# RG-LRU layer of a four-layer trunk: another form of the input scale, later gates, and one weight pool for the whole layer

## The chip, the core and the metric

The kernel runs on one core of a Trainium2 chip. The metric is the device time of one launch in microseconds (us), taken as the median of several runs. The engines are named as in the profile: PE (TensorE, matrix multiplication), PEld (its weight loads), DVE (VectorE), ACT (ScalarE), POOL (GpSimd), and SP, whose queue issues all the DMAs of this kernel.

## The reference

One step of a trunk with four layers and 384 tokens (128 of context, then 256 latents), width 1024. Each layer is a token mixer, a normalisation, a gated ConvFFN and another normalisation. The mixers are gated DeltaNet (layers 0 and 3), Mamba-2 SSD (layer 1) and RG-LRU (layer 2). Everything is float32. The change touches layer 2's mixer, whose core is:

```
def lru_mixer(h, s0, w_in, w_conv, conv_b, gate_w, gate_b, lam, w_out):
    gate_branch, xr = jnp.split(h @ w_in, 2, axis=-1)              # 1280 channels each
    xr = dwconv1d(xr, w_conv) + conv_b                             # 4 taps along the tokens
    gates = jnp.einsum('btnk,dgnkm->btdgnm', xr.reshape(b, t, 10, 128), gate_w)
    gates = jax.nn.sigmoid(gates.reshape(b, t, 2, 2, 1280) + gate_b)
    r, i = gates[:, :, :, 0], gates[:, :, :, 1]                    # for two directions
    log_a = -8.0 * r * jax.nn.softplus(-lam)
    bx = jnp.sqrt(-jnp.expm1(2.0 * log_a)) * i * xr[:, :, None]
    a = jnp.exp(log_a)
    y, s_fin = bidirectional(linear_scan, (a fwd, bx fwd), (a bwd, bx bwd), s0)   # h = a h + bx
    y = y * jax.nn.gelu(gate_branch)
    return y @ w_out, s_fin
```

The kernel before writes 1 - a^2 as (1 + a^2) tanh(-log a), and the kernel after takes its root from (1 + a)^2 tanh(-log(a)/2).

## The kernel before

**Number format and weights.** Every float32 product is made of three matmuls on halves: a weight `w` becomes `wh` (rounded, written by ACT at L111) and `wl = raw - wh` (POOL or DVE at L120), and the activations are split in the same way. `wload` does it: a DMA into a `raw` tile, the ACT copy, the subtraction. A pool on the right side of the memory holds a number of `raw` tiles and of `wh`/`wl` pairs. `WBUFS` gives these two numbers for the mixers of kind 0, 1 and 2 (gated DeltaNet, SSD, RG-LRU), and its last entry is for the output projection and the FFN. SSD has 3 `raw` tiles and 4 pairs, RG-LRU has 4 and 3. The loads of the modulation weights (`ada`, 512 KB each) that run beside the mixer take tiles of the same `raw` ring.

**Order.** The program is written for a framework that places the tiles, sets the semaphores and orders the instructions of each engine by the program order and by its own estimates of time; once made, each engine's order is fixed and runs in sequence. `keep_in_program_order` pins some ACT instructions.

**The mixer `lru`.** Ten blocks of 128 channels. `proj` goes through 20 projections of 24 matmuls of 128x384: x0-x3, z0-z2, x4-x6, z3-z5, x7-x9, z6-z9, each into one of two banks of accumulators `psc`. For an x block, `conv4` (one ACT instruction, then six of DVE at L117) makes `xr`, which is split into `xh` and `xl`; for a z block a copy brings it into `gb` (DVE at L765). `proj` yields four times per projection, and at each yield the generators in `post` go one step. `gates(n, ...)` waits two steps, then makes four gate products of three matmuls each, with sigmoids by ACT into `R` (the r gates) and `Iv` (the i gates), and multiplies `Iv` by `xr`, on POOL for odd n.

After each group of x blocks `scans` runs: `decay(n)` makes tanh and exp of `log a` on ACT (pinned), then on DVE and POOL the product (1 + a^2) tanh(-log a) in `th`; ACT takes the root; `scan(n)` multiplies `Iv` by `th`, runs four scans (L688), copies the final states into `st` (L691) and adds the two directions. When the z blocks of the group are there, a GELU on `gb` and a product give y.

**Output projection.** `outproj` multiplies the split y (`yh`, `yl`) with ten weights, k = 0 to 9. The first three weights are loaded at the end of `proj` from the mixer's own pool; then this pool is closed and another, `WBUFS[3]` = (2, 6), is opened for the rest of the layer. The last four k wait in `late` and are multiplied token tile by token tile in `boundary`, together with the normalisation. Before that, four weights of the FFN are fetched ahead from the same pool. Only y0 is split into a tile of the outer pool; the others have six `yh`/`yl` pairs of a pool that is opened when the mixer's inner pool has been closed.

Of the kernel before, what the change touches and what calls it, by code (L numbers as in the profile page):

```python
# [9 lines left out]
AF = mybir.ActivationFunctionType  # L10
ALU = mybir.AluOpType
# [4 lines left out]
NT = 384  # L16
# [9 lines left out]
SIDE = 4, 4, 4  # L26
FENCE = 4
HOSTED = ((6, 2, 1), (3, 2, 1), (3, 0, 1), (2, 1, 0))
WBUFS = ((4, 2), (3, 4), (4, 3), (2, 6))


C_ID, C_MU, C_ML, C_SG = 0, 128, 256, 384
# [52 lines left out]
class Trunk:  # L85
# [425 lines left out]
    def outw(self, wsrc, k):  # L511
        return self.wload(wsrc[k], lo_eng=self.nc.vector if k % 2 else self.nc.gpsimd)

    def outproj(self, l, nk, wsrc, gety, tail=4, ws=(), swap=False):

        pts = self.acc6()
        late, y = [], gety(0)
        for k in range(nk):
            if k == nk - tail - 1:
                self.open_bnd(l, 0)  # L520
            w = ws[k] if k < len(ws) else self.outw(wsrc, k)
            nxt = gety(k + 1) if k + 1 < nk else None
            if k < nk - tail:
                for t in range(3):
                    for half in range(2):
                        self.out_mm(pts[t][half], t, half, w, y, k == 0, False)
            else:
                late.append((k, w, y))
            if swap and k == len(ws) - 1:
                self.close_w()  # L530
                self.open_w(*WBUFS[3])
            y = nxt
        self.prefetch([self.I["ffn_in"][l, i % 2 * NFF + i // 2] for i in range(4)])
        self.boundary(l, 0, pts, late, nk)
# [18 lines left out]
    def ffn(self, l):  # L553
# [3 lines left out]
        with tc.tile_pool(name=self.nm("ffn"), bufs=1, reuse_waits="tile") as fp:  # L557
# [57 lines left out]
            if not last:  # L615
                self.open_w(*WBUFS[self.next_layer(l) % 3])
                self.prefetch(self.first_srcs(self.next_layer(l)))
# [3 lines left out]
    def lru(self, l, j):  # L621
        nc, tc, I = self.nc, self.tc, self.I
        NB = 10
        done, post = set(), []
        with ExitStack() as es:
            op = es.enter_context(tc.tile_pool(name=self.nm("lru"), bufs=1, reuse_waits="tile"))
            Iv = self.sb(op, [128, NB, 2, NT], "I")
            gb = self.sb(op, [128, NB, NT], "gb")
            flat = gb.rearrange("p n t -> p (n t)")
            lpool = tc.tile_pool(name=self.nm("lru1"), bufs=1, reuse_waits="tile")  # L630
            lp = self.adap = lpool.__enter__()
            cw = self.sb(op, [128, NB, 5], "cw")
            sm = self.sb(op, [128, NB, 8], "sm")
            sa = self.sb(op, [128, NB, 2], "sa")
            st = self.sb(op, [128, NB, 2], "st")
            R = None

            def small():
                self.load(cw, I["lru_conv"])
                self.load(sm, I["lru_small"])  # L640
                nl = self.sb(op, [128, NB, 2], "nl")
                self.ts(nl, sm[:, :, 4:6], -1.0, ALU.mult)
                out = []
                for _ in self.softplus(op, nl, [128, NB, 2], "sp", out):
                    pass
                sp = out[0]
                self.ts(sa, sp, -8.0, ALU.mult)

            def gates(n, xr, xs, wg):
                for _ in range(2):  # L650
                    yield
                for q in range(4):
                    s = slice(q * 128, (q + 1) * 128)
                    pg = self.ps("b")
                    self.mm3(pg[:, :NT], (wg[0][:, s], wg[1][:, s]), xs, True, True)
                    dst = (R, Iv)[q % 2][:, n, q // 2, :]
                    self.act(dst, pg[:, :NT], AF.Sigmoid, 1.0, sm[:, n, q:q + 1])
                    yield
                iv = Iv[:, n, :, :]
                self.tt(iv, iv, xr.unsqueeze(1).to_broadcast([128, 2, NT]), ALU.mult, (nc.vector, nc.gpsimd)[n % 2])  # L660
                done.add(("gate", n))

            ths, ys = {}, []

            def gety(pool, n, bufs):
                yh, yl = (self.sb(pool, [128, NT], t, bufs, F32R) for t in ("yh", "yl"))
                self.split(yh, yl, Iv[:, n, 0, :])
                return yh, yl

            def decay(n):  # L670
                r = R[:, n, :, :]
                th = ths[n] = self.sb(lp, [128, 2, NT], "th", 4)
                for f in (AF.Tanh, AF.Exp):
                    for d in range(2):
                        dst = th if f == AF.Tanh else r
                        tc.keep_in_program_order(self.act(dst[:, d, :], r[:, d, :], f, sa[:, n, d:d + 1]))
                u = self.sb(lp, [128, 2, NT], "u", 2)
                self.ts(th, th, -1.0, ALU.mult, 1e-30, ALU.max)
                self.tt(u, r, r, ALU.mult, nc.gpsimd)
                self.stt(th, u, 1.0, th, ALU.add, ALU.mult)  # L680

            def scan(n):
                r, iv = R[:, n, :, :], Iv[:, n, :, :]
                self.tt(iv, iv, ths[n], ALU.mult)
                for d in range(2):
                    for si, (a, b) in enumerate(SEGS):
                        rng = slice(a, b) if d == 0 else slice(b - 1, a - 1 if a else None, -1)
                        nc.vector.tensor_tensor_scan(  # L688
                            out=iv[:, d, rng], data0=r[:, d, rng], data1=iv[:, d, rng],
                            initial=sm[:, n, 6 + d:7 + d] if si else 0.0, op0=ALU.mult, op1=ALU.add)  # L690
                nc.vector.tensor_copy(st[:, n, :], iv.rearrange("p d t -> p (d t)")[:, 127:NT + 1:NT - 127])  # L691
                self.tt(iv[:, 0, :], iv[:, 0, :], iv[:, 1, :], ALU.add)

            def scans(ns, zs):
                while not all(x in done for x in [("gate", n) for n in ns] + [("scan", n) for n in range(ns[0])]):
                    yield
                for n in ns:
                    decay(n)
                    yield
                    yield  # L700
                for n in ns:
                    tc.keep_in_program_order(self.act(ths[n], ths[n], AF.Sqrt))
                    yield
                for n in ns:
                    scan(n)
                    done.add(("scan", n))
                    yield
                while ("z", zs[-1]) not in done:
                    yield
                g = gb[:, zs[0]:zs[-1] + 1, :]  # L710
                tc.keep_in_program_order(self.act(g, g, AF.Gelu_apprx_tanh))
                for n in zs:
                    y = Iv[:, n, 0, :]
                    self.tt(y, y, gb[:, n, :], ALU.mult)
                    if n == 0:
                        ys.append(gety(op, 0, 1))
                    yield

            def proj():
                nonlocal R  # L720
                parts = (range(4), range(3)), (range(4, 7), range(3, 6)), (range(7, NB), range(6, NB))
                seq = [(k, n) for p in parts for k, ns in zip("xz", p) for n in ns]
                lo = nc.gpsimd, nc.vector
                first = self.first_pair([I["lru_in"][NB + k] for k in range(2)])
                small()
                affine = self.affine(flat[:, :D], flat[:, D:2 * D])
# [4 lines left out]

                def gate_w(n):
                    if n < NB:
                        return self.wload(I["lru_gate"][n], 512, ("gwh", "gwl"), 2, lp, lo[n % 2])

                gw, nxt = gate_w(0), None
                for i, (kind, n) in enumerate(seq):
                    w = nxt
                    if i < 2:
                        pt = first[i]  # L740
                        if i:
                            nxt = weights(2)
                    else:
                        pt = self.ps("c")[:, :NT]
# [7 lines left out]
                    for _ in range(2):  # L752
                        next(affine, 0)
                    if kind == "x":
                        xr = self.sb(lp, [128, NT], "xr", 3)
                        self.conv4(pt, xr, cw[:, n, 0:4], cw[:, n, 4:5])
                        xh = self.sb(lp, [128, NT], "xh", 3, F32R)
                        xl = self.sb(lp, [128, NT], "xl", 3, F32R)
                        self.split(xh, xl, xr)
                        if R is None:  # L760
                            R = self.sb(lp, [128, NB, 2, NT], "R")
                        post.append(gates(n, xr, (xh, xl), gw))
                        gw = gate_w(n + 1)
                    else:
                        nc.vector.tensor_copy(gb[:, n, :], pt)  # L765
                        done.add(("z", n))
                    for ns, zs in parts:
                        if (kind, n) == ("x", ns[-1]):
# [2 lines left out]
                while self.fillers:  # L771
                    self.fill()
                    yield
                for k in range(3):
                    ws.append(self.outw(I["lru_out"], k))
                self.close_h()

            ws = []
            self.interleave([], proj(), post, [], None, done, 1.0, None)
            lpool.__exit__(None, None, None)  # L780
            kpool = es.enter_context(tc.tile_pool(name=self.nm("lru2"), bufs=1, reuse_waits="tile"))
            self.outproj(l, NB, I["lru_out"], lambda n: gety(kpool, n, 6) if n else ys[0], ws=ws, swap=True)
            with tc.issue_after(self.last_load.ins):
                self.load(self.O["lru"], st)

# [1032 lines left out]
```

## Time and profile before

| What | Value |
|---|---|
| Time, median of 3 runs | 2821.39 us (2820.75 to 2823.31) |
| The profiled execution | 2822.25 us, its span 2820.5 us |
| PE, PEld busy | 2603.0 us (92%), 2315.0 us (82%) |
| DVE, ACT, POOL busy | 1968.2 us (70%), 1328.0 us (47%), 1302.6 us (46%) |
| Granted clock of TensorE, mean | 0.968 |
| Layer 2's mixer, from its first matmul to the FFN's first | 1512.5 to 1765.2 us of the span |

The busy times are sums over stages that differ. An engine's row in the chain of waits, or what a wait of PE ended on, tells more than its share. A line such as L117 is that of a helper which records one kind of operation for the whole kernel (L105 a matmul, L111 an activation, L117 scalar_tensor_tensor, L120 tensor_tensor, L124 tensor_scalar, L134 a DMA), so the tile names tell what a row is. In a list of groups the columns are: engine, operation, out<-in, shape, count, then busy time in all and mean ns of one, then the idle time of the engine ahead of them and what ended it.

### The profile page before, as it was taken

The numbers are of one execution on the slowest core, as the hardware profiler recorded it, in microseconds if no ns is written. First come the engines' busy times: TensorE is split into PE (matmuls) and PEld (weight loads), VectorE is DVE, ScalarE is ACT, GpSimd is POOL, SyncE is SP. The second block draws the span as 40 slices with busy tenths as digits, with TensorE's granted clock in tenths as the row PEclk, the third lists the DMA queues.
The fourth block names the chain that finished last, engine by engine and source line by source line (L and its number), as shares of the span: only waits on it lengthen the run. The fifth ranks groups of instructions, "written<-read, shape, count | busy, mean of one in ns | idle before, by whom it ended". The sixth has DMA issues, their size and how long they took to land. (4 is left out here: it accounts for less than half of the span.)

```text
span 2820.5 us, 43591 instructions
## 1 busy us (share of the span) xinstructions
PE 2603.0 (92%) x16376; PEld 2315.0 (82%) x16376; DVE 1968.2 (70%) x4240; ACT 1328.0 (47%) x2304; POOL 1302.6 (46%) x730
## 2 busy tenths in 40 slices
PE   6899999999989998999998777999979999899997
PEld 3798887799977887779997675899969989778996
DVE  3766655787787676378777776787776665578777
ACT  2456545434335566343434564344345555544443
POOL 1443432456544334345664653456546434335663
PEclk8999999999999999999999998999999999899998
DMA  7532314544444342554445443334442112153442
GB/s 256 177 100 92 111 63 161 174 130 135 149 163 152 119 129 78 187 169 135 136 144 170 156 140 111 119 127 138 160 144 90 53 59 62 36 185 121 150 134 84
DMA packets 114643, 366.47 MB, mean 130 GB/s; under 512 B 13760, under 2 KB 25728, under 8 KB 114432
## 3 DMA queue, kind: packets, MB, share of 16 engines
q1 hardware_dynamic: 114432, 363.67, 39.9%
q8 instruction: 130, 2.13, 0.3%
q14 instruction: 81, 0.66, 0.1%
HBM read 357.78 MB, written 5.84 MB: 129 GB/s over the span
## 5 line engine op out<-in xcount | busy, mean ns | idle before, releaser
L120 POOL TENSOR_TENSOR wl<-raw,wh 128x1024 fp32r<-128x1024 f32 x305 | 737.5, 2428 | 858.1 <-ACT wh L111 821.8
L105 PE MATMUL psc<-hh,wh 128*128 128x384 f32 x2168 | 759.9, 351 | 55.7 <-DVE xr L117 16.2
L117 DVE SCALAR_TENSOR_TENSOR acc<-psc,cw,acc 128x189 f32<-128x189 f32 (+3 forms) x1680 | 646.2, 412 | 164.6 <-ACT acc L111 131.2
L105 PE MATMUL psc<-hh,wl 128*128 128x384 f32 x2168 | 738.1, 340 | 3.4 <-POOL wl L120 3.4
L105 PE MATMUL psc<-hl,wh 128*128 128x384 f32 x2168 | 735.8, 339 | 0.0
L105 PEld LDWEIGHTS psc<-hh,wh 128*128 128x128 f32 x2168 | 413.8, 191 | 100.8 <-issue 69.7
L111 ACT ACTIVATE wh<-raw 128x1024 fp32r<-128x1024 f32 x345 | 362.4, 1053 | 264.9 <-PE psc L105 51.2
L105 PEld LDWEIGHTS psc<-hl,wh 128*128 128x128 f32 x2168 | 414.5, 191 | 5.7 <-issue 2.4
L105 PEld LDWEIGHTS psc<-hh,wl 128*128 128x128 f32 x2168 | 412.9, 190 | 7.0 <-POOL wl L120 5.1
L120 POOL TENSOR_TENSOR wol<-raw,woh 128x1024 fp32r<-128x1024 f32 x88 | 211.8, 2407 | 160.9 <-ACT woh L111 159.8
L111 ACT ACTIVATE gh<-g 128x384 fp32r<-128x384 f32 x88 | 46.2, 525 | 329.0 <-DVE g L120 329.0
L111 ACT ACTIVATE acc<-psc,cw 128x384 f32<-128x384 f32 x168 | 96.6, 575 | 191.7 <-PE psc L105 191.7
L120 POOL TENSOR_TENSOR PB<-M,cst 128x512 fp32r<-128x512 f32 x96 | 128.2, 1350 | 112.1 <-PE psa L105 110.1
L111 ACT ACTIVATE V<-psa 128x512 fp32r<-128x512 f32 x144 | 84.9, 595 | 133.7 <-PE psa L105 133.2
L105 PE MATMUL psa<-woh,gl 128*128 128x512 f32 x352 | 137.1, 391 | 3.6 <-DVE gl L120 3.6
L105 PE MATMUL psa<-woh,gh 128*128 128x512 f32 x352 | 137.5, 391 | 0.2 <-ACT gh L111 0.2
L105 PE MATMUL psa<-wol,gh 128*128 128x512 f32 x352 | 137.6, 391 | 0.0
L105 PE MATMUL psa<-raw,csilu 128*32 128x256 f32 x1216 | 106.4, 418 | 28.3 <-DMA raw<-in_ada_w 28.1
L111 ACT ACT_TABLE_LOAD x66 | 84.7, 1283 | 36.0 <-DVE kT L117 12.0
L120 DVE TENSOR_TENSOR wl<-raw,wh 128x1024 fp32r<-128x1024 f32 x40 | 54.3, 1358 | 59.2 <-ACT wh L111 58.9
L111 ACT ACTIVATE woh<-raw 128x1024 fp32r<-128x1024 f32 x88 | 92.6, 1052 | 0.0
L120 DVE TENSOR_TENSOR gl<-g,gh 128x384 fp32r<-128x384 f32 x88 | 53.7, 610 | 52.3 <-ACT gh L111 52.3
(341 smaller groups left out, 5163.3 us busy)
## 6 DMA issues: line engine op xcount, KB each, us to landing
raw<-in_ffn_in SPq DMA_DIRECT2D x176, 512.0 KB
raw<-in_ada_w SPq DMA_DIRECT2D x152, 512.0 KB
raw<-in_ffn_out SPq DMA_DIRECT2D x88, 512.0 KB
raw<-in_gdn_in SPq DMA_DIRECT2D x66, 512.0 KB
araw<-in_ada_w SPq DMA_DIRECT2D x40, 512.0 KB
raw<-in_ssd_in SPq DMA_DIRECT2D x25, 512.0 KB
raw<-in_lru_in SPq DMA_DIRECT2D x20, 512.0 KB
raw<-in_gdn_out SPq DMA_DIRECT2D x16, 512.0 KB
```

What stands on the lines that cost most here:

```text
L105: return self.nc.tensor.matmul(out, l, r, start=start, stop=stop, skip_group_check=True)
L111: x = self.nc.scalar.activation(out, in_, f, scale=scale, bias=bias, **kw)
L117: return self.nc.vector.scalar_tensor_tensor(out=out, in0=a, scalar=s, in1=b, op0=op0, op1=op1)
L120: return (eng or self.nc.vector).tensor_tensor(out=out, in0=a, in1=b, op=op)
```

## The change

Six edits to layer 2's mixer:

1. `decay` takes tanh(-log(a)/2) with a second column of factors `sh`, and multiplies `Iv` by (1 + a) itself. The negation with its lower bound (L124), the square `u` on POOL and the product with `th` go; the root is taken of the tanh alone.
2. The z blocks are copied by ACT, not DVE.
3. `gates` begins four steps behind its projection, not two. `R` is a ring of seven tiles of one block instead of one tile for all, and `xr` has two tiles, not three.
4. `Iv` times `xr` is on DVE for every block; the lower halves of the gate weights are on POOL for every block; the copy into `st` is on POOL.
5. y0, y1 and y2 are split into tiles of the outer pool as soon as they are made.
6. RG-LRU's pool has 3 `raw` tiles and 5 pairs and is kept to the end of the layer, the FFN included (`swap` is gone); four output weights are fetched at the end of `proj`, not three.

```diff
-WBUFS = ((4, 2), (3, 4), (4, 3), (2, 6))
+WBUFS = ((4, 2), (3, 4), (3, 5), (2, 6))
...
-            if swap and k == len(ws) - 1:
-                self.close_w()
-                self.open_w(*WBUFS[3])
             y = nxt
...
                 self.ts(sa, sp, -8.0, ALU.mult)
+                self.ts(sh, sp, 4.0, ALU.mult)
 
             def gates(n, xr, xs, wg):
-                for _ in range(2):
+                for _ in range(4):
                     yield
+                R[n] = self.sb(lp, [128, 2, NT], "R", 7)
...
-                self.tt(iv, iv, xr.unsqueeze(1).to_broadcast([128, 2, NT]), ALU.mult, (nc.vector, nc.gpsimd)[n % 2])
+                self.tt(iv, iv, xr.unsqueeze(1).to_broadcast([128, 2, NT]), ALU.mult)
...
             def decay(n):
-                r = R[:, n, :, :]
+                r, iv = R[n], Iv[:, n, :, :]
                 th = ths[n] = self.sb(lp, [128, 2, NT], "th", 4)
-                for f in (AF.Tanh, AF.Exp):
-                    for d in range(2):
-                        dst = th if f == AF.Tanh else r
-                        tc.keep_in_program_order(self.act(dst[:, d, :], r[:, d, :], f, sa[:, n, d:d + 1]))
-                u = self.sb(lp, [128, 2, NT], "u", 2)
-                self.ts(th, th, -1.0, ALU.mult, 1e-30, ALU.max)
-                self.tt(u, r, r, ALU.mult, nc.gpsimd)
-                self.stt(th, u, 1.0, th, ALU.add, ALU.mult)
+                for d in range(2):
+                    tc.keep_in_program_order(self.act(th[:, d, :], r[:, d, :], AF.Tanh, sh[:, n, d:d + 1]))
+                for d in range(2):
+                    tc.keep_in_program_order(self.act(r[:, d, :], r[:, d, :], AF.Exp, sa[:, n, d:d + 1]))
+                self.stt(iv, r, 1.0, iv, ALU.add, ALU.mult)
...
-                nc.vector.tensor_copy(st[:, n, :], iv.rearrange("p d t -> p (d t)")[:, 127:NT + 1:NT - 127])
+                nc.gpsimd.tensor_copy(st[:, n, :], iv.rearrange("p d t -> p (d t)")[:, 127:NT + 1:NT - 127])
                 self.tt(iv[:, 0, :], iv[:, 0, :], iv[:, 1, :], ALU.add)
...
-                    if n == 0:
-                        ys.append(gety(op, 0, 1))
+                    if n < 3:
+                        ys[n] = gety(op, n, 3)
...
-                        return self.wload(I["lru_gate"][n], 512, ("gwh", "gwl"), 2, lp, lo[n % 2])
+                        return self.wload(I["lru_gate"][n], 512, ("gwh", "gwl"), 2, lp)
...
-                        xr = self.sb(lp, [128, NT], "xr", 3)
+                        xr = self.sb(lp, [128, NT], "xr", 2)
...
-                        if R is None:
-                            R = self.sb(lp, [128, NB, 2, NT], "R")
...
-                        nc.vector.tensor_copy(gb[:, n, :], pt)
+                        self.act(gb[:, n, :], pt, AF.Copy)
...
-                for k in range(3):
+                for k in range(4):
                     ws.append(self.outw(I["lru_out"], k))
...
-            self.outproj(l, NB, I["lru_out"], lambda n: gety(kpool, n, 6) if n else ys[0], ws=ws, swap=True)
+            self.outproj(l, NB, I["lru_out"], lambda n: ys.get(n) or gety(kpool, n, 6), ws=ws)
```

More of the change, by code (lines that the diff above doesn't have):

```diff
@@ L512, in outw, with outproj @@
         return self.wload(wsrc[k], lo_eng=self.nc.vector if k % 2 else self.nc.gpsimd)
-    def outproj(self, l, nk, wsrc, gety, tail=4, ws=(), swap=False):
+    def outproj(self, l, nk, wsrc, gety, tail=4, ws=()):
         pts = self.acc6()
@@ L634, in lru @@
             sa = self.sb(op, [128, NB, 2], "sa")
+            sh = self.sb(op, [128, NB, 2], "sh")
             st = self.sb(op, [128, NB, 2], "st")
-            R = None
+            R = {}
             def small():
@@ L655, in gates @@
                     self.mm3(pg[:, :NT], (wg[0][:, s], wg[1][:, s]), xs, True, True)
-                    dst = (R, Iv)[q % 2][:, n, q // 2, :]
+                    dst = Iv[:, n, q // 2, :] if q % 2 else R[n][:, q // 2, :]
                     self.act(dst, pg[:, :NT], AF.Sigmoid, 1.0, sm[:, n, q:q + 1])
@@ L659, in gates @@
                 iv = Iv[:, n, :, :]
-                self.tt(iv, iv, xr.unsqueeze(1).to_broadcast([128, 2, NT]), ALU.mult, (nc.vector, nc.gpsimd)[n % 2])
+                self.tt(iv, iv, xr.unsqueeze(1).to_broadcast([128, 2, NT]), ALU.mult)
                 done.add(("gate", n))
-            ths, ys = {}, []
+            ths, ys = {}, {}
             def gety(pool, n, bufs):
@@ L670, in decay @@
             def decay(n):
-                r = R[:, n, :, :]
+                r, iv = R[n], Iv[:, n, :, :]
                 th = ths[n] = self.sb(lp, [128, 2, NT], "th", 4)
-                for f in (AF.Tanh, AF.Exp):
-                    for d in range(2):
-                        dst = th if f == AF.Tanh else r
-                        tc.keep_in_program_order(self.act(dst[:, d, :], r[:, d, :], f, sa[:, n, d:d + 1]))
-                u = self.sb(lp, [128, 2, NT], "u", 2)
-                self.ts(th, th, -1.0, ALU.mult, 1e-30, ALU.max)
-                self.tt(u, r, r, ALU.mult, nc.gpsimd)
-                self.stt(th, u, 1.0, th, ALU.add, ALU.mult)
+                for d in range(2):
[3 more added lines that the diff above has]
+                self.stt(iv, r, 1.0, iv, ALU.add, ALU.mult)
             def scan(n):
-                r, iv = R[:, n, :, :], Iv[:, n, :, :]
+                r, iv = R[n], Iv[:, n, :, :]
                 self.tt(iv, iv, ths[n], ALU.mult)
@@ L714, in scans @@
                     self.tt(y, y, gb[:, n, :], ALU.mult)
-                    if n == 0:
-                        ys.append(gety(op, 0, 1))
+                    if n < 3:
+                        ys[n] = gety(op, n, 3)
                     yield
             def proj():
-                nonlocal R
                 parts = (range(4), range(3)), (range(4, 7), range(3, 6)), (range(7, NB), range(6, NB))
                 seq = [(k, n) for p in parts for k, ns in zip("xz", p) for n in ns]
-                lo = nc.gpsimd, nc.vector
                 first = self.first_pair([I["lru_in"][NB + k] for k in range(2)])
```

## The prediction

> **What bounds the kernel now.** I read the busy times by stage first, then what PE waited for in each stage, then the chain of work that ended last, then the groups. The stage table is for the whole mixer and four parts of it; its columns are busy time (and count) of PE, PEld, DVE, ACT and POOL, then TensorE's granted clock.
>
> ```profile
> core 0: us, PE busy (x) PEld busy (x) DVE busy (x) ACT busy (x) POOL busy (x), PEclk, DMA share, GB/s
> 1537.00:1708.00 171.00, 129.56 (x728) 109.32 (x726) 131.31 (x186) 104.34 (x156) 95.10 (x47) 0.92 0.43 139
> 1571.00:1624.00 53.00, 35.21 (x207) 29.68 (x205) 48.60 (x67) 32.65 (x48) 31.50 (x16) 0.94 0.44 137
> 1624.00:1667.00 43.00, 33.80 (x202) 29.33 (x202) 35.79 (x52) 27.96 (x40) 22.13 (x10) 0.92 0.51 161
> 1690.00:1708.00 18.00, 10.19 (x30) 7.04 (x29) 18.00 (x28) 9.01 (x12) 5.09 (x2) 0.77 0.23 81
> 1708.00:1749.00 41.00, 37.28 (x139) 28.74 (x139) 17.34 (x22) 12.31 (x14) 12.11 (x5) 0.89 0.41 132
> ```
>
> The reader is to see that DVE is all but full from 1571 to 1624 (48.6 of 53) and wholly full from 1690 to 1708, while PE stands at two thirds and about half. The chain of waits between 1571 and 1710 says the same: the scans, the products on `I` and the two operations on `th` lead it, all on DVE.
>
> ```profile
> by line: DVE I L688 19.2%; DVE I L120 15.4%; DVE th L117 11.4%; DVE th L124 7.2%; DVE xr L117 6.8%; POOL wl L120 4.2%; PE psb L105 4.1%; DVE st L691 3.5%; POOL u L120 3.4%; DVE gwl L120 3.3%; PE psc L105 3.3%; DVE xl L120 3.2%; DMA raw<-in_
> ```
>
> So what the mixer can gain is what PE waits for. First from 1571 to 1690 (the projections), then from 1690 to 1749 (the output projection); the columns are the total, the times and the longest.
>
> ```profile
> PE psc L105 <- DVE xr L117: 16.2, 5, 5.1
> PE psb L105 <- DVE xl L120: 5.4, 2, 3.8
> PE psc L105 <- POOL wl L120: 3.0, 2, 2.8
> PE psc L105 <- DVE gb L765: 2.7, 2, 2.5
> ```
>
> ```profile
> PE psa L105 <- DVE yl L120: 5.0, 1, 5.0
> PE psa L105 <- ACT wh L111: 3.1, 2, 1.8
> PE psa L105 <- POOL wl L120: 2.7, 2, 1.7
> ```
>
> Together 27.3 us in the first and 10.8 us in the second. To these comes time at a lower clock: length times (1 - clock) is 3.2 and 3.4 us in the second and third rows of the table, 4.1 and 4.5 us in the last two, 15.2 us at most, since part of it was idle anyhow.
>
> **The work that is removed and moved.** The groups on DVE and POOL from 1537 to 1708:
>
> ```profile
> L117 DVE SCALAR_TENSOR_TENSOR th<-u,th 128x768 f32<-128x768 f32 x10 | 17.9, 1794 | 5.7 <-POOL u L120 5.3
> ...
> L124 DVE TENSOR_SCALAR th<-th 128x768 f32<-128x768 f32 x10 | 14.4, 1435 | 13.2 <-ACT th L111 13.1
> ...
> L120 DVE TENSOR_TENSOR I<-I,xr 128x768 f32<-128x768 f32 x5 | 6.7, 1348 | 6.7 <-ACT I L111 6.6
> L120 DVE TENSOR_TENSOR gwl<-raw,gwh 128x512 fp32r<-128x512 f32 x4 | 6.6, 1651 | 0.0
> L120 DVE TENSOR_TENSOR I<-I 128x384 f32<-128x384 f32 x10 | 6.3, 630 | 0.0
> L691 DVE COPY st<-I 128x2 f32<-128x2 f32 x10 | 5.7, 565 | 0.0
> L765 DVE COPY gb<-psc 128x384 f32<-128x384 f32 x10 | 5.5, 548 | 1.4 <-PE psc L105 1.4
> ```
>
> ```profile
> L120 POOL TENSOR_TENSOR u<-R 128x768 f32<-128x768 f32 x10 | 16.7, 1670 | 6.4 <-ACT R L111 6.4
> L120 POOL TENSOR_TENSOR x<-x,gb 128x512 f32<-128x512 f32 x9 | 13.8, 1553 | 0.0
> L120 POOL TENSOR_TENSOR I<-I,xr 128x768 f32<-128x768 f32 x5 | 11.6, 2327 | 4.7 <-ACT I L111 4.7
> L120 POOL TENSOR_TENSOR gwl<-raw,gwh 128x512 fp32r<-128x512 f32 x4 | 6.6, 1657 | 3.8 <-ACT gwh L111 3.8
> ```
>
> DVE loses the negation (14.4), the gate weights' lower halves (6.6), the state copies (5.7) and the z copies (5.5), 32.2 us, and gains five products with `xr` at 1.35, 6.7 us. The product (1 + a) on `Iv` has the count and shape of the one on `th` that goes. Net 25.5 of 131.3 us, a fifth. The views of the tiles `th` and `st` give minimum, median and maximum in ns:
>
> ```profile
> L124 DVE TENSOR_SCALAR th<-th x10: 548/1466/2756, 1571.5 to 1688.1; 128x768 f32<-128x768 f32 x10
> L117 DVE SCALAR_TENSOR_TENSOR th<-u,th x10: 943/2018/2944, 1575.5 to 1689.0; 128x768 f32<-128x768 f32 x10
> ```
>
> ```profile
> L691 DVE COPY st<-I x10: 132/136/2286, 1598.7 to 1705.2; 128x2 f32<-128x2 f32 x10
> ```
>
> A copy of two elements takes 0.13 or 2.29 us: the long ones stand behind POOL's work. So POOL's load counts twice. It loses 28.3 us (`u` and its products with `xr`) and gains some 7 us of gate weights and ten tiny copies. Without `u` the new product may fall from 1.79 to 0.94 us, 8.5 us more; I count none of that apart.
>
> **Terms in the projections, 1571 to 1690.**
> - The `xr` waits (16.2 us): PE lacks an accumulator bank because `conv4` stands in DVE's queue behind the `th` chain and the scans. Between nothing and 16.2; a fifth of DVE's work goes, and the rounds ACT-DVE-POOL-DVE-ACT ahead of the root too, so I take 10.
> - The `xl` waits (5.4): with four steps, about one projection, between split and gate products, I take 5. Each gate ends two steps later; behind the last come four z projections, which hide that for PE.
> - The z copies (2.7): ACT frees the bank now, but in its own queue. Nearest row, an ACT read of the same shape from PSUM:
>
> ```profile
> L111 ACT ACTIVATE R<-psb,sm 128x384 f32<-128x384 f32 x20 | 11.4, 576 | 16.3 <-PE psb L105 16.1
> ```
>
>  ten times 0.58 is 5.8 us on an engine with 104.3 of 171 busy; between -2.7 and +5.8, I take -2, as the row is as short as DVE's.
> - POOL's `wl` (3.0): POOL is lighter by about 20 of 95 us; I take 1.
> - Clock: 3 of the 6.6 us here.
>
> That is -21.
>
> **The price of three `raw` tiles.** This speaks against the change. Loads issued between 1518 and 1674.4 us:
>
> ```profile
> raw<-in_ada_w SPq DMA_DIRECT2D x22, 512.0 KB
> raw<-in_lru_in SPq DMA_DIRECT2D x18, 512.0 KB
> raw<-in_lru_gate SPq DMA_DIRECT2D x8, 256.0 KB
> ```
>
> 48 loads in 156.4 us through four tiles: a tile is held for up to 13.0 us (DMA, ACT's copy, POOL's subtraction, and any wait for a free pair). With three, the same length needs 9.8 us. The SSD mixer has three, and from 855 to 899 us, 44 us long, it issued 16 full loads:
>
> ```profile
> raw<-in_ssd_in SPq DMA_DIRECT2D x9, 512.0 KB
> raw<-in_ada_w SPq DMA_DIRECT2D x7, 512.0 KB
> ```
>
> 2.75 us a load, a hold of 8.25. At that pace the 48 loads take 132 us (no price); at an unchanged hold 208 us (+52). The SSD row is the nearer, since two more pairs let a `raw` tile go earlier; but POOL is busier here. I take +5, counting the first projections (1512 to 1571), where nothing else changes for PE. The projections thus gain 16.
>
> **Terms in the output projection, 1690 to 1749.** Before, the second pool held everything up:
>
> ```profile
> 1719.23 13.64 SPq L134 DMA_DIRECT2D raw<-in_lru_out  x5
> ```
>
> ```profile
> 1716.47 0.52 ACT L111 ACTIVATE yh<-I 128x384 fp32r<-128x384 f32 x1 [4.84 <-PE psb L105]
> 1716.90 1.99 ACT L111 ACTIVATE wh<-raw 128x1024 fp32r<-128x1024 f32 x2
> ```
>
> The last five loads start at 1719.2, after ACT, stuck behind a `yh` copy, has made the halves of k = 3 and 4. After the change three y are ready when the z blocks end, four weights are on their way, and no pool changes. `yl` goes (-5.0), ACT's `wh` too (-3.1), POOL's `wl` by half (-1.4), the clock gives 3 of 8.6: -12.5. The last scans get hardly shorter (their ACT part is the same) but PE has k = 0 to 5 meanwhile.
>
> **Costs.** The state copy on POOL reads what the following add overwrites, so each add on DVE waits for POOL. No row shows such a copy on POOL; bounds are DVE's 0.13 us and POOL's smallest product here, 1.55, and a wait behind POOL's queue. Other scans stand in between; only the last of a group is exposed: +1. With five pairs, of which `late` holds four, one FFN weight of the first two is split only after the last product: between 0, hidden by the last token tile's normalisation, and 3.6 us (1.05 ACT + 2.5 POOL): +1. In the FFN, five pairs for one in use leave a lead of four projections: 0; without that lead each weight would show its 3.6 us.
>
> **Sum.** -21 + 5 - 12.5 + 2 = -26.5 us. The profiled execution took 2822.25 us (span 2820.5), the median is 2821.39; I predict 2821.4 - 26.5 = **2795 us**.
>
> The Trainium skill (TensorE: Matmul & The Clock Gate, Part 1: The HAM clock gate) says that an idle window of about 3.4 us halves PE's clock, and that about 3.4 us of work bring it back. By it only the waits of 5.1, 3.8 and 5.0 us would have cost clock, 1.7 us each, an estimate of 5.1 us instead of my 6, and 2796 us. The trace's 0.77 after the 5.0 us wait agrees in direction.
>
> **Rivals.**
> 1. Slower: the load ring decides. For: each `raw` tile was in use to the end, and POOL makes all gate halves. If the hold falls only to 11 us, 48 x 11 / 3 = 176 us, 20 more than now where I count 16 less: 2795 + 36 = 2831. It decides above a hold of 10.4 us. Against: SSD's 8.25.
> 2. Half the gain: ACT becomes the bound. 104.3 + 5.8 = 110.1 us; if ACT cannot be busier than 65% (27.96 of 43 in the third row), the 171 us become 169, -2 in place of -16: 2809. Against: nothing but the dependencies holds ACT at 65%.
> 3. More: all PE waits (38.1) and all lost clock (15.2) go, for PE is then the bound: 2821.4 - 53.3 + 5 = 2773; nine tenths of the way 2778.
> 4. It does nothing: the adds wait 2 us each behind POOL's 2.5 us `wl`, ten times on the chain, and 20 of 26.5 us are gone: 2816 to 2821.
>
> **Chances.** Forecast (2784 to 2804) 0.55; rival 2 0.16; rival 3 0.12; rival 4 0.08; slower 0.09. The range 2775 to 2815 leaves out the slower case, rival 4, and the edge of rival 3. A change of 0.2%, 5.6 us, is about what this kernel's measurement can tell. Faster 0.83, within 0.2% 0.08, slower 0.09.
>
> **What would show it.** `xr` and `xl` waits of PE below 7 us together; no `yl` wait above 1 us; the clock above 0.95 in the output projection; DVE near 105 us for the projections. It is wrong if PE waits for DMAs of `raw` by more than 10 us (rival 1), for ACT (rival 2), or DVE's adds wait for POOL (rival 4).

## The result, and the profile after

| | Before | After |
|---|---|---|
| Median of the runs | 2822.35 us (2820.75 to 2827.51) | 2807.84 us (2801.15 to 2809.66) |
| Ratio | | 0.994, 95% interval 0.9928 to 0.9953 |
| The profiled execution (span) | 2822.25 us (2820.5) | 2801.15 us (2799.3) |
| Mixer, first matmul to the FFN's first | 252.7 us | 230.0 us |

Faster, by 14.5 us where 26.5 were forecast, and inside the stated range. The ratio is not simply the quotient of the two medians (0.9949), which lies inside its interval. In a second set of runs the changed kernel had a median of 2802.57 us against 2821.89, with the same ratio of 0.994 (0.9927 to 0.9952). The profiled execution of after is the fastest of its runs, 6.7 us below their median, so sizes below are read within that execution, and a difference of 2 to 3 us between two traces is no finding: two executions of the changed kernel have 170.1 and 172.4 us for the projections.

I divide the mixer at the last projection matmul (z9). Stage table of before, then of after; the columns are those of the prediction's first fence, the first row is the projections, the second runs to the FFN's first matmul.

```profile
1512.50:1689.80 177.30, 140.98 (x882) 120.35 (x878) 133.84 (x206) 105.15 (x160) 99.88 (x51) 0.94 0.48 154
1689.80:1765.20 75.40, 53.11 (x199) 39.59 (x197) 50.01 (x75) 33.08 (x48) 24.81 (x11) 0.86 0.34 108
```

```profile
1513.20:1683.30 170.10, 140.85 (x882) 119.36 (x879) 99.44 (x183) 110.04 (x171) 83.80 (x49) 0.92 0.51 164
1683.30:1743.20 59.90, 46.49 (x199) 36.55 (x197) 49.38 (x68) 33.22 (x49) 31.68 (x14) 0.90 0.42 136
```

The projections lost 7.2 us, the second stage 15.5, together 22.7; the two profiled executions differ by 21.1, so the rest of the program took 1.6 us more. The forecast had the larger part in the projections, 16 us, and 10.5 after them. DVE lost a quarter of its work in the projections (133.84 to 99.44), and PE's 882 instructions take the same 141 us. So what changed there is PE's waiting. First three rows of before that the prediction did not show (three more, of 0.2 to 1.1 us, are left out, and `xl` is 5.6 us over the whole stage), then all the rows of after, each over its first stage:

```profile
PE psa L105 <- DMA raw<-in_ada_w: 4.6, 3, 3.2
...
PE psb L105 <- ACT R L111: 1.5, 1, 1.5
...
PE psb L105 <- ACT xh L111: 0.9, 1, 0.9
```

```profile
PE psa L105 <- DMA raw<-in_ada_w: 16.4, 8, 7.1
PE psc L105 <- DVE xr L117: 6.4, 3, 5.0
PE psc L105 <- POOL wl L120: 2.8, 2, 1.8
PE psb L105 <- DVE xl L120: 2.0, 2, 1.7
PE psc L108 <- DVE adab L120: 0.5, 1, 0.5
PE psa L108 <- DVE x L124: 0.5, 1, 0.5
PE psc L105 <- ACT wh L111: 0.4, 1, 0.4
```

The sum of all such rows is 36.3 us before and 29.0 after: 7.3 less, as the stage. The reader is to see two movements against each other: all other waits fell by 19.1 us, and the wait for loads of the modulation weights, which the change does not touch, rose from 4.6 to 16.4.

After z9, the same view of before (the two larger rows not shown yet) and of after:

```profile
PE psc L108 <- ACT x L111: 6.9, 2, 3.8
...
PE psb L105 <- DVE hh L382: 3.8, 1, 3.8
```

```profile
PE psa L105 <- DVE yl L120: 5.7, 1, 5.7
PE psb L105 <- DVE hh L382: 4.4, 1, 4.4
PE psc L108 <- ACT x L111: 3.3, 1, 3.3
```

Waits fell from 22.3 to 13.4 us, and PE's own time for the same 199 instructions from 53.1 to 46.5 at a clock of 0.90 instead of 0.86: 8.9 and 6.6 make the 15.5.

Where the longest load wait comes from can be followed in the order of time (columns: start, duration, engine, operation, count, and in brackets the idle time before and what ended it):

```profile
1536.23 0.33 SPq L134 DMA_DIRECT2D raw<-in_lru_gate  x1
...
1547.95 1.15 ACT L111 ACTIVATE gwh<-raw 128x512 fp32r<-128x512 f32 x2 [0.85 <-PE psb L105]
1548.66 2.49 POOL L120 TENSOR_TENSOR gwl<-raw,gwh 128x512 fp32r<-128x512 f32 x2 [5.89 <-ACT gwh L111]
...
1549.95 0.33 SPq L134 DMA_DIRECT2D raw<-in_lru_gate  x1
...
1551.17 3.34 SPq L134 DMA_DIRECT2D raw<-in_ada_w  x2
...
1555.63 1.08 PE L105 MATMUL psa<-raw,csilu 128*32 128x256 f32 x8 [7.07 <-DMA raw<-in_ada_w]
```

A gate weight was asked for at 1536.2 (the one before it at 1530.1), but ACT can split it only when PE has finished the gates of an earlier block and a pair is free: 1548. Two of three `raw` tiles hold these weights for 15 and 20 us. The first that POOL frees, at 1549.95, goes to the next gate weight in the queue; only with the second, at 1551.17, are the next modulation weights issued, and PE, whose instructions run in order, stands for 7 us.

### The profile page after: what moved, and what is told of

It reads as the page before. It is cut to its first block, busy times and chain, and to the rows that moved or that the text cites. A ratio compares the mean times of both kernels' runs of the same rounds, so it can differ in the third digit from the quotient of the medians.

```text
span 2799.3 us, 43568 instructions
## 1 busy us (share of the span) xinstructions
PE 2596.3 (93%) x16376; PEld 2312.1 (83%) x16376; DVE 1934.0 (69%) x4211; ACT 1333.2 (48%) x2315; POOL 1292.6 (46%) x730
## 5 line engine op out<-in xcount | busy, mean ns | idle before, releaser
L111 ACT ACT_TABLE_LOAD x67 | 86.0, 1283 | 35.5 <-DVE kT L117 11.8
L105 PEld LDWEIGHTS psa<-raw,csilu 128*32 128x32 f32 x1216 | 28.9, 112 | 82.3 <-DMA raw<-in_ada_w 47.6
```

Source lines behind the costliest of these rows:

```text
L105: return self.nc.tensor.matmul(out, l, r, start=start, stop=stop, skip_group_check=True)
L111: x = self.nc.scalar.activation(out, in_, f, scale=scale, bias=bias, **kw)
```

## The experiments

The theories. A: it is the four-step lag that keeps the gate weights' pairs, blocks the ring and makes loads late. B: three `raw` tiles are too few whatever the lag. C: the load waits only take the place of other waits, and the projections are as long without them. The table has all runs; "projections" and "after z9" are the two stages in the profiled execution, "waits" the sum of PE's waits in the projections, "loads" that part of it which ended on a modulation weight's DMA. A ratio is taken against the runs of before in the same set (their medians lie between 2820.65 and 2822.71 us); the row "before" has one of these sets.

| Kernel | Median us | Ratio (95%) | Projections | After z9 | Waits | Loads |
|---|---|---|---|---|---|---|
| before | 2821.89 | 1 | 177.3 | 75.4 | 36.3 | 4.6 |
| after, again | 2802.57 | 0.9940 (0.9927-0.9952) | 172.4 | 60.4 | 28.4 | 14.5 |
| math alone | 2814.76 | 0.9976 (0.9964-0.9987) | 166.0 | 74.1 | 25.3 | 6.8 |
| old pool | 2812.90 | 0.9966 (0.9955-0.9978) | 172.0 | 67.8 | 25.9 | 11.3 |
| z on DVE | 2805.89 | 0.9938 (0.9926-0.9950) | 168.1 | 64.2 | 26.8 | 13.4 |
| lag of two | 2799.82 | 0.9929 (0.9916-0.9941) | 168.0 | 59.2 | 21.6 | 5.6 |
| four raw, four pairs | 2802.63 | 0.9941 (0.9927-0.9955) | 170.3 | 62.1 | 28.1 | 11.9 |
| three gate pairs, R 5 | 2813.93 | 0.9968 (0.9957-0.9980) | 176.6 | 63.9 | 32.2 | 17.3 |
| R 5 alone | 2800.58 | 0.9925 (0.9912-0.9938) | 169.9 | 59.9 | 29.2 | 15.2 |
| late request | 2805.81 | 0.9944 (0.9930-0.9958) | 170.4 | 61.7 | 28.4 | 6.6 |
| late request, three pairs, R 5 | 2800.57 | 0.9934 (0.9921-0.9947) | 167.7 | 61.4 | 27.1 | 5.7 |
| lag of two, xr 3, R 5 | 2802.54 | 0.9938 (0.9922-0.9954) | 167.7 | 59.3 | 25.2 | 6.6 |
| lag of two, scans spread, R 5 | 2803.75 | 0.9936 (0.9924-0.9947) | 174.1 | 58.3 | 26.9 | 5.3 |

**The changed kernel again**, for the noise. No edit.

> The changed kernel once more, unaltered, for its spread: its four runs lay between 2801.2 and 2809.7 us, and the profiled one was the fastest. If the spread is that of single executions, five more runs fall into the same 8 us, and another profile shows the same order of waits: about 17 us of PE waiting for modulation loads in the mixer, 5.7 us for yl. If the profile shown was an exception, a second one shows a stage that is 6 to 8 us longer, and tells which.

The ratio repeats; the load waits are 14.5 us here.

**The mathematics alone**: the kernel before with only edit 1 (the factors `sh` come with it).

```diff
...
-                self.ts(th, th, -1.0, ALU.mult, 1e-30, ALU.max)
-                self.tt(u, r, r, ALU.mult, nc.gpsimd)
-                self.stt(th, u, 1.0, th, ALU.add, ALU.mult)
+                self.stt(iv, r, 1.0, iv, ALU.add, ALU.mult)
...
```

> The kernel before with the new form of the scale alone: tanh of half the argument, the root of it, (1 + a) on Iv; no negation, no square on POOL; all else as before, with 4 raw tiles, the two-step lag and the second pool. By the prediction's terms DVE loses 14.4 us and POOL 16.7 us, and the xr waits of 16.2 us fall by about half: 8 us faster than before. If the DVE queue was the whole limit in the projections: 12 us or more. If the removed work lay beside other work: within 3 us of before.

Its waits over the projections, and its stages:

```profile
PE psc L105 <- DVE xr L117: 9.4, 4, 3.1
PE psa L105 <- DMA raw<-in_ada_w: 6.8, 4, 3.1
PE psb L105 <- DVE xl L120: 5.7, 4, 3.8
```

```profile
1511.80:1677.80 166.00, 140.22 (x882) 120.07 (x878) 117.49 (x198) 105.05 (x161) 79.15 (x41) 0.94 0.51 165
1677.80:1751.90 74.10, 52.68 (x198) 39.82 (x196) 47.02 (x73) 32.39 (x48) 25.08 (x11) 0.86 0.34 110
```

Edit 1 alone gives 7 us of time, about as expected, and in its trace the shortest projections of all kernels, 166.0: next to the two traces of the changed kernel the other five edits together add some 4 to 6 us to that stage. How much exactly is not shown, since the profiled execution took 2809.64 us, 5.1 us less than this kernel's median. It gives 1.3 us after z9.

**The old pool**: the changed kernel with edit 6 undone; the early splits stay.

```diff
-WBUFS = ((4, 2), (3, 4), (3, 5), (2, 6))
+WBUFS = ((4, 2), (3, 4), (4, 3), (2, 6))
...
+            if swap and k == len(ws) - 1:
+                self.close_w()
+                self.open_w(*WBUFS[3])
...
-                for k in range(4):
+                for k in range(3):
...
```

> The changed kernel with the weight pool's edit undone: (4, 3) tiles, the pool closed and opened inside the output projection as before, three output weights ahead instead of four. The three early splits stay. My reading of the two traces is that the output projection's gain (from the last projection matmul to the feed-forward's first pair 75.5 us before, 59.9 after) comes from the output weights that are there in time: then this run has 72 to 76 us there again and the wait for wh and wl is back, while the projections, with four raw tiles, lose load waits (17 to about 7 us) and gain 4 to 6 us; in sum 2807 to 2813. Rival: the gain comes from the early splits of y; then the output projection stays at 60 to 64 us and the time is 2796 to 2800.

```profile
1516.60:1688.60 172.00, 146.09 (x881) 124.53 (x878) 103.03 (x182) 115.67 (x174) 81.02 (x48) 0.90 0.49 159
1688.60:1756.40 67.80, 51.85 (x199) 39.98 (x197) 46.51 (x68) 34.10 (x50) 28.41 (x14) 0.85 0.38 120
```

```profile
PE psc L108 <- ACT x L111: 5.6, 2, 3.8
PE psb L105 <- DVE hh L382: 3.2, 1, 3.2
PE psa L105 <- ACT wh L111: 2.7, 1, 2.7
PE psa L105 <- POOL wl L120: 2.3, 2, 1.9
PE psa L105 <- DVE wl L120: 2.2, 1, 2.2
```

Neither reading was right alone. After z9 it is 74.1 us with edit 1 alone, 67.8 with 2 to 5 as well (the early splits among them) and 59.9 with the pool too: the two steps are worth 6 and 8 us there. The waits for `wh` and `wl` (7.2 us) are back here and no `yl` wait stands in the rows; in the changed kernel it is the reverse. The four `raw` tiles, which I had expected to give 4 to 6 us back in the projections, give nothing there: the load waits fall to 11.3 us only, and the stage takes 172.0. In time, edit 1 alone is worth 0.24%, and to take edit 6 back costs 0.26%, both more than the intervals allow for chance; if such shares add, which no run shows, they are most of the 0.6% of all six.

**z on DVE**: edit 2 undone.

```diff
-                        self.act(gb[:, n, :], pt, AF.Copy)
+                        nc.vector.tensor_copy(gb[:, n, :], pt)
```

> The changed kernel with the copies of z out of PSUM on VectorE as before. The prediction took 2 us of gain for them on ScalarE. If that is so, 2804 to 2807 and xr or xl waits up by about 2 us; if VectorE has that time free by now (16.9 us idle near 1550 us), the same time within 1.5 us; if ScalarE's copies delay Sigmoids that VectorE waits for, 1 to 3 us faster than the changed kernel.

The ratio is 0.9938 against 0.9940: the edit is worth nothing that can be told. The median lies where the first reading had it, but the `xr` and `xl` waits are 6.3 us, not more than the 8.4 of the changed kernel. That DVE had the time free fits the trace, in which it stands idle for 15.9 us up to 1554.4, but is not shown by it.

**A lag of two**, and **four raw tiles with four pairs**: each one number of the changed kernel.

```diff
-                for _ in range(4):
+                for _ in range(2):
```

> The changed kernel with gates two steps behind instead of four (xr keeps its two tiles). Theory A: four steps hold the two gate-weight pairs longer, so the next gate weight waits unsplit in one of the three raw tiles, and the modulation loads come late. Then this gives back most of the 7.1 us wait near 1550 us of the span; the xl waits return with 2 to 4 us; net 4 to 8 us faster than the changed kernel. Theory B: three raw tiles are too few whatever the lag. Then the waits for modulation loads stay near 17 us and the xl waits make it 2 to 5 us slower than the changed kernel. Theory C, that loads do not set the time: no difference beyond 2 us.

> The changed kernel with 4 raw tiles and 4 weight pairs in place of 3 and 5. Theories A and B alike: PE's waits for modulation loads fall from 17 us to about the 5.6 us of the kernel before, the projections get 6 to 10 us shorter; with four pairs all held by the last four k, the FFN's first weights come later and cost 1 to 6 us; net 2 to 8 us faster than the changed kernel. Theory C: no gain, or slower by the cost at the FFN's start.

With the shorter lag the load waits fall to 5.6 us with three `raw` tiles; with the long lag and four tiles they are still 11.9. That speaks for A against B, and for neither against C. The lag of two has the lowest sum of waits:

```profile
PE psa L105 <- DMA raw<-in_ada_w: 5.6, 6, 1.9
PE psc L105 <- POOL wl L120: 4.1, 5, 1.1
PE psb L105 <- DVE xl L120: 3.6, 4, 1.5
PE psc L105 <- DVE xr L117: 3.4, 2, 3.2
```

But of the 7.4 us of waits only 2.1 are gone from the stage, since PE's busy time in it is 146.1 us instead of 140.9. The mean clock (0.93 and 0.92) doesn't say why. By groups, the 220 modulation matmuls have 21.6 us instead of 18.9 of it; the cause stays open. Its time can't be told from that of the changed kernel: the intervals overlap.

**Three gate pairs**, with five `R` tiles to make room, and **five R tiles alone** as its control.

```diff
-                R[n] = self.sb(lp, [128, 2, NT], "R", 7)
+                R[n] = self.sb(lp, [128, 2, NT], "R", 5)
...
-                        return self.wload(I["lru_gate"][n], 512, ("gwh", "gwl"), 2, lp)
+                        return self.wload(I["lru_gate"][n], 512, ("gwh", "gwl"), 3, lp)
```

> The changed kernel with three pairs of gate-weight tiles (gwh, gwl) instead of two; to make the room, the ring of R tiles has five instead of seven. The lag of four steps and the three raw tiles stay. Theory A (with the long lag a pair of gate weights is held for more than two blocks, the next gate weight lies unsplit in one of the three raw tiles, and the load behind it is issued late): TensorE's waits for loads in the projections fall from 17.0 us to 6 or below, the 7.1 us wait near 1555 us is gone, and the time falls 5 to 8 us below that of the changed kernel, to about 2796. Theory B (three raw tiles are too few whatever the lag): the waits for loads stay at 12 us or more and the time at that of the changed kernel. Theory C (the waits for loads only take the place of others): the waits fall, but xr and xl waits rise by as much and the time stays.

> The control of the run with three gate-weight pairs: the changed kernel with a ring of five R tiles instead of seven and nothing else. If a ring of five holds up the gates' Sigmoids (the sixth block's R must wait for the first block's scan), ScalarE's waits for R appear and the time rises by 2 to 6 us; if not, time and waits are those of the changed kernel within 1.5 us (TensorE's load waits 14 to 17 us in the projections).

Theory A in this form fell. Five `R` tiles cost nothing; a third pair took no load wait away (17.3 us against 15.2) and made the kernel slower than its control. The trace shows why the loads stay late: the third gate weight is split early, at 1535, and so the queue simply runs on to the next ones. They were issued at 1537.65 and 1547.43, and both were split only when PE had finished the first gates, at 1554.2 and 1555.7:

```profile
1537.65 0.37 SPq L134 DMA_DIRECT2D raw<-in_lru_gate  x1
...
1547.43 0.33 SPq L134 DMA_DIRECT2D raw<-in_lru_gate  x1
1554.12 4.74 SPq L134 DMA_DIRECT2D raw<-in_ada_w  x2
```

The rest of its loss (a load wait of 7.2 us at 1625, a clock of 0.89) I can't put down to one thing.

**The late request**, with two pairs and with three (and five `R` tiles). The gates ask for their weights themselves, two steps before use; blocks 0 and 1 are as before (`gate_w` moves up in the code for this).

```diff
-                for _ in range(4):
+                for s in range(4):
+                    if s == 2 and n > 1:
+                        wg = gate_w(n)
                     yield
...
-                        gw = gate_w(n + 1)
+                        gw = gate_w(1) if n == 0 else None
...
```

> The changed kernel, lag of four and two pairs of gate weights, with the gate weights of blocks 2 to 9 requested by the gates themselves two steps before use, instead of by the projection one block and more before. Third pair gave nothing (load waits 9.2 us before 1577 against 9.7 in its control), because the load queue runs ahead and lets two gate weights lie unsplit in raw tiles whatever the number of pairs. Theory A2 (it is the order of the requests that blocks the ring): load waits in the projections fall from 17 (changed kernel) to 5 to 9 us, xr and xl stay near 8, the time falls 4 to 8 us, to 2795 to 2799. Theory B (three tiles are too few whatever the order): load waits stay at 12 or more, time 2801 to 2806. Rival D: now the gate weights themselves come late; TensorE waits for gwh and gwl 3 us or more, and the time does not fall.

> The late request of the run beside it with three pairs of gate weights and five R tiles (the ring of five alone left time and waits as they were). Theory A2: no gate weight lies in a raw tile for a released pair, load waits at 4 to 7 us, no wait for gwh or gwl, time 2793 to 2798, not above the late request with two pairs by more than 2 us. If the request time matters less than the pairs, it is the run with three pairs again: load waits 15 us or more and about 2812.

The waits of the first over the projections:

```profile
PE psc L105 <- DVE xr L117: 10.8, 2, 5.6
PE psa L105 <- DMA raw<-in_ada_w: 6.6, 2, 4.9
PE psb L105 <- ACT I L111: 3.8, 1, 3.8
PE psb L105 <- POOL gwl L120: 2.3, 1, 2.3
PE psb L105 <- DVE xl L120: 1.8, 2, 1.3
PE psb L105 <- ACT R L111: 1.3, 1, 1.3
```

This bears out A2 for the waits and C for the time. The order of the requests is the cause of the late loads: with lag, tiles and pairs as they were, 16.4 us become 6.6. And it is worth nothing that can be told: waits for `xr`, for ACT's Sigmoids and for `gwl` come up, the sum is 28.4 as against 29.0, and the stage has its 170 us. With three pairs it is 27.1 us of waits, and 0.9934 against the control's 0.9925.

**Three xr tiles** on the lag of two, with five `R` tiles:

```diff
-                        xr = self.sb(lp, [128, NT], "xr", 2)
+                        xr = self.sb(lp, [128, NT], "xr", 3)
```

> The changed kernel with a lag of two steps and three xr tiles (five R tiles make the room, which alone left the time as it was). The prediction went by the xr waits (16.2 us before) and did not see that the change takes xr from three tiles to two, so that a block's convolution waits for the gates' last product two blocks earlier. If that holds conv4 up: xr and xl waits in the projections fall from 7.0 us (lag of two, two tiles) to 4 or less and the time 2 to 4 us below that of the lag of two, to about 2796. If not (conv4 waits for the PSUM pass, not for xr): the same waits and 2798 to 2801.

The wait of 3.2 us in the first panel, which the lag of two has with two tiles, is gone; one of 5.1 us stands at 1644 instead, and the time didn't fall.

**The scans spread**: a second `yield` after each scan, with the lag of two and five `R` tiles.

> The changed kernel with a lag of two, five R tiles, and the scans of a panel two steps apart instead of one. In five of the kernels so far one wait of about 5 to 6 us for xr stands near 1640 to 1652, where VectorE does the second panel's scans (some 12 us together) before the last block's convolution. Theory E (that pile of scans is what keeps the projections at 168 to 172 us, whatever else is taken away): the largest xr wait after 1625 falls below 2 us, the projections come to 163 to 166 us and the time to 2794 to 2798. Theory C (each wait removed gives way to another): the sum of TensorE's waits in the projections stays at 25 to 30 us, the projections at 167 to 170, and the time at 2798 to 2802, that of the lag of two. Against both: the scans end later, the last panel's multiplies with z and the output projection start late, and the output projection takes 2 to 4 us more (63 instead of 59).

```profile
PE psc L105 <- DVE xr L117: 7.9, 2, 4.7
PE psc L105 <- POOL wl L120: 7.6, 7, 3.1
PE psa L105 <- DMA raw<-in_ada_w: 5.3, 5, 1.6
```

Theory E fell: an `xr` wait of 4.7 us stands after 1625, where the lag of two by itself has none, `wl` waits came up, and the stage has 174.1 us. DVE's order there is hardly changed, so the run moved less than it was meant to.

Taken together, in eight variants of the changed kernel's loads, lag and tiles the load waits lie between 5.3 and 17.3 us, while in six of them the sum of waits is 25 to 30 us, and in six the projections take 167.7 to 170.4. No version is faster than the changed kernel by more than the intervals tell. Which chain keeps the stage there stays open.

## Why the prediction was right or wrong

The time lies in the stated range of 2775 to 2815 us; of the narrower forecast, 2784 to 2804, it is outside in the first set of runs and inside in the second. That is in part luck: the projections gave 8.8 us less than was said and the output projection 5.0 us more, and the two misses partly cancel. Of the four signs that the prediction named, only DVE's work came as said; the `xr` and `xl` waits make 8.4 us, not less than 7, the `yl` wait is 5.7 us and the clock 0.90. And a sign against it, more than 10 us of waits for `raw` loads, is there with 16.4.

- **DVE holds PE up in the projections: right, by the waits.** Its work in the forecast's window came to 105.6 us, where "near 105" was said (columns as in the stage tables):

```profile
1537.00:1708.00 171.00, 138.99 (x779) 116.77 (x778) 105.61 (x167) 116.84 (x176) 86.72 (x48) 0.90 0.49 157
```

  That the figure fits so well is again luck in part, since the same window holds other work after the change. Over the whole mixer DVE lost 35.0 us, not 25.5; the new product took 1.04 us on average instead of 1.79, a gain of 7.5 us that the prediction named and did not count.

  The `xr` waits fell by 9.8 (said: 10), the `xl` waits by 3.6 (5), those for the z copies by 2.7 (2), those for `wl` by 0.2 (1), and those for ACT's `R` and `xh` by 2.4, which I had not counted: 18.7 against 18. But whether these are five causes is another matter: edit 1 alone shortened the stage by 11.3 us in its trace, and z on ACT, to which I gave 2, is worth nothing that can be told.
- **The price of three raw tiles: the step that failed.** I took +5; the load waits rose by 11.8. The mean gives no hint of it: 49 loads were issued between 1519 and 1668 us, 3.04 us a load, so a tile is held for up to 9.1 us, between SSD's 8.25 and the 10.4 at which rival 1 decides. But such a mean is the length of the stage over its loads, and can't tell whether the ring sets that length; to price the ring by it was the error. Two tiles held for 15 and 20 us at one place cost PE 7 us. I had costed edit 3 by what waits on `xl`, and not by what its longer lag holds: the gate weights' pairs, the `raw` tile behind them, and `xr`, now with two tiles. The runs show the order of requests as the cause; they also show that to take the wait away buys no time that can be told, so the 6.8 us that the term was short explain the sum of the trace, and not, by themselves, the time.
- **The clock in the projections: wrong.** I took 3 us; it went from 0.94 to 0.92 and PE's time stayed at 141 us. The estimate of 5.1 us counted three waits and left out a fourth, of 3.65 us (it ended at 1606.84), which totals and longest waits do not show; four would make 6.8. And the 0.77 belongs to the row that ends with the 5.0 us wait, at 1708.14, not to what follows: from 1708 to 1712 the clock is 0.50.
- **The output projection: right in sum, wrong inside.** I said 12.5, less 2 of costs; 15.5 came. `wh` and `wl` went as said (`wl` wholly, 2.7). The `yl` wait did not go, against "no `yl` wait above 1 us": y3 to y5 now stand behind the last scans on DVE, and it is 5.7 us. The clock gave twice my 3 us (53.1 to 46.5 us for the same matmuls), though 0.90 over the stage, and 0.93 up to 1734, isn't the 0.95 I named; and an ACT `x` wait fell by 3.6. By the runs, the step of edits 2 to 5, with the early splits, and that of the pool have about equal parts.
- **The state copy on POOL: right to be small.** The copy takes 0.56 us, and no instruction waits for it (the last row has nothing under it):

```profile
L689 POOL COPY st<-I x10: 432/561/567, 1596.0 to 1699.8; 128x2 f32<-128x2 f32 x10
...
who waited for it (us, times):
```

- **The rivals.** 1 (the ring decides) had its sign right, more than 10 us of load waits, and its outcome wrong. 2 (ACT becomes the bound, 2809) comes nearest by the number; ACT's work in the projections rose by 4.9 us (5.8 said) and fills 65% of the stage, the share that it supposed as the most. But only 0.4 us of PE's waits end on ACT, so the changed kernel doesn't show its mechanism; with the late request 5.1 us do. 3 and 4 fell.

## What to carry to other kernels

Cost a longer lag by everything that is held meanwhile, along the whole chain: here the pair, the staging tile behind the pair, and with it the one queue that feeds a quite different consumer. The mean hold of a ring doesn't tell what it costs; look for the one tile that is held for twice the mean. And a wait that is taken away is a gain only if the next one on the same engine isn't due at the same time: price the stage from an experiment that moves one edit, since terms read from one trace's waits don't add.

## What the runs showed of the hardware

PE ran at half pace for some time after some gaps in its work. Eight identical modulation matmuls took 0.64 us after a gap of 3.02 us and 1.08 us after the next, of 3.96 (the kernel with three gate pairs, in order of time):

```profile
1557.85 0.64 PE L105 MATMUL psa<-raw,csilu 128*32 128x256 f32 x8 [3.02 <-DMA raw<-in_ada_w]
1562.45 1.08 PE L105 MATMUL psa<-raw,csilu 128*32 128x256 f32 x8 [3.96 <-DMA raw<-in_ada_w]
```

The first matmuls behind a gap don't tell, though, whether it costs clock, for the half pace can begin later. In the kernel before, after the wait of 3.65 us, matmuls of 128x384 took 0.34 us at first, and 0.53 us each from 1608.2 to 1611.1. In the kernel with z on DVE the same eight took 0.64 us after a gap of only 1.83 us (at 1613.85), and from 1615.1 to 1617.8 matmuls of 128x384 took 0.52 us or more.

The Trainium skill (TensorE: Matmul & The Clock Gate, Part 1: The HAM clock gate) puts the idle window that throttles at about 3.4 us. The two lines lie on either side of it, but the runs don't bear it out as a limit: the eight took 1.08 us also after a gap of 3.23 us (the kernel before, at 1554.49) and, in the lag of two, after one of only 1.86 us. What decides it stays open.

```profile
1614.38 1.08 PE L105 MATMUL psa<-raw,csilu 128*32 128x256 f32 x8 [1.86 <-DMA raw<-in_ada_w]
```
